# First three attention steps placed among the last value products, modulation terms spread, and separate places for stacked q and k

## The chip, the core and the metric

The kernel runs on one core of a Trainium2 chip. A core has TensorE (PE; its weight loads are listed as PEld), VectorE (DVE), ScalarE (ACT), GpSimd (POOL) and SyncE (SP), which here issues all DMAs. The metric is device time in microseconds (us) of one execution, as a median of several; less is better.

## What is computed

One layer of a backbone block over 512 latent tokens and 256 context tokens, width 1024, all in fp32:

```
sh1, sc1, g1, sh2, sc2, g2 = split(silu(c) @ w_mod + b_mod, 6)
h, hc = modulate(rms_norm(x), sh1, sc1), modulate(rms_norm(ctx), csh1, csc1)
qa, ka, va, hy, qd, kd, vd = split(h @ w_in)          # context rows: k and v only
yd = (softmax(q1 k1) - lam * softmax(q2 k2)) vd       # 4 heads, two components of 64
ya = softmax(qa ka) va                                # 4 query heads on 2 key heads
yh = x2 * conv(h2, x1 * conv(h1, v))                  # long convolutions of 256 channels
x = x + g1 * (concat(rms_norm each of ya, yh, yd) @ w_out)
x = x + g2 * ((gelu(dwconv3(a)) * v) @ w_down)        # a, v = split(modulate(rms_norm(x), sh2, sc2) @ w_up)
```

Queries are 512 rows, keys 768 (256 of the context, 512 latent). The last four parts of the modulation vector (g1, sh2, sc2, g2) are needed only behind the attention.

## The kernel before

**Numbers.** Nearly every product is three matmuls (lines 80 to 83): an operand is split into a high part (ScalarE cast, line 70) and a low remainder (line 78), and hi*hi, hi*lo and lo*hi are summed in PSUM. Scores do it in two matmuls: q and k are transposed to one row per channel, and their high and low halves are stacked along the 128 partitions, so that `ks` (high k twice) and `kz` (low k beside zeros) each need one pass.

**Stages.** Modulation and filters; Hyena projection and convolutions; the q, k and v projections, eight chunks of 256 columns (line 722, `corder`), chunks 6 and 7 the values of the differential heads; attention; output projection; feed-forward. A chunk has two halves of the contraction (`u`), and in each half a block of 12 matmuls for every 128 rows (`b`, `j`): chunk 7 has twelve such blocks.

**Orders.** Outside the blocks marked `manual_schedule` a planner orders each engine's instructions by its own model of time, so an engine's order need not be that of the program. Inside such a block the named engines keep the order of the program. The attention is such a block for TensorE, VectorE and ScalarE (line 1067); the projections are not. Every engine works its list strictly in order, SP's DMA issues included.

**Modulation terms.** Each of the four later parts is a group of eight terms: `mod2_step` (line 694) loads 512 KB of `w_mod` and adds them to `macc` (VectorE, lines 706 and 708; two load buffers, one accumulator). The call after a group's eighth term does the column sums (`due`, 16 small matmuls, line 713, into `mc`) and goes on with the next group. Three groups run beside the projections, two calls ahead of each half chunk from the fourth on (line 730), and the fourth beside the feed-forward stage.

**Preparation of a head.** `prepare` (line 662) transposes q and k, splits them, and stacks them by DMA on SP: four transfers of 128 KB for q (lines 614 to 617) and four of 192 KB for k (line 654). Head 0 is prepared ahead of chunk 6, into the tiles that later hold the attention's outputs (`y`); the others during the attention. There the unstacked q and the unstacked k of a head share one buffer (tag `qk`, lines 608 and 630).

**Attention steps.** A step is 128 queries of one head; the differential heads have four steps each and two score tiles per step. Step n does its scores (`front`: lines 831 and 832, then maximum on VectorE, line 837, and exponential on ScalarE, line 839), mixes the two components of step n - 1 (`combine`, POOL lines 976 and 977), transposes the probabilities of step n - 3 and multiplies those of step n - 5 by the values. Head i + 1 is prepared from the steps in `PREP_AT`; the two Hyena outputs (`y_out`) are transposed at `HY_AT`. The output weights (`wo_unit`, line 1032) go through three raw tiles, tag `wr`, which the projections used before.

In PSUM (8 banks) the projections have three banks of tag `a`, three of `t`, and two of `p`, used by the early modulation and filters and then by the convolution (lines 112 and 516).

## Time and profile before

| | us |
|---|---|
| median of 3 runs | 823.11 (821.0 to 825.92) |
| the profiled execution | 824.9 |
| its span, first to last instruction | 823.1 |
| mean granted TensorE clock | 0.987 of full speed |

The span is what the engines' rows cover; 1.8 us of the execution lie around it. In a timeline row stand start, duration, engine, line of the kernel, operation, output and inputs, shape, and in brackets how long the engine was idle ahead of it and what ended that. Tile names carry their use: `q7L`, `q7C` are the sums of chunk 7 (latent and context rows), `sd02` the scores of head 0, query block 2, `mxd..` their maxima, `pd..` the exponentials, `Td..` the transposes, `yd` the products with the values; `qTd`, `kT0d` the transposes of q and k, `qhld`, `khd` their unstacked halves, `qsd`, `ksd` the stacked ones; `mraw` is a modulation load. Names leave buffer numbers out, and a matmul's row lasts longer than the distance to the next, since matmuls overlap.

### The profile page before, as it was taken

To read this page: it belongs to the slowest core of one execution; us is meant where nothing else is said; L and a number is where in the kernel's file an instruction comes from. 1 tells how busy PE (TensorE), PEld (TensorE's weight loads), DVE (VectorE), ACT (ScalarE), POOL (GpSimd) and SP (SyncE) were. 2 spreads that over 40 slices of the span, in tenths; PEclk is the share of its full clock that TensorE was granted. 3 is DMA by queue.
4 is the path that set the end of the run, shared out by engine and by line. 5 is a ranking of instruction groups with operands and counts; after the bars stand their busy time and mean duration, and the time that the engine had idled before them with its cause. 6 is when DMAs were issued, how large, how long until landed. Compare 5 with 4: busy or idle time off the path is not lost.

```text
span 823.1 us, 11104 instructions
## 1 busy us (share of the span) xinstructions
PE 780.4 (95%) x4334; PEld 657.2 (80%) x4334; DVE 479.3 (58%) x679; ACT 318.6 (39%) x546; POOL 204.0 (25%) x190
## 2 busy tenths in 40 slices
PE   5878999999999788899999999999999999999997
PEld 1247899999999677699888988888888888888886
DVE  4855578886766677678477595344443334333325
ACT  1554424323221477678444263323332233322320
POOL 0652406848841267613043000000000000000000
PEclk9998999999999899999999999999999999999999
DMA  8902232124668232212073173332223233232202
GB/s 326 382 1 88 67 127 78 52 78 137 217 232 247 57 81 57 64 26 78 27 256 105 46 260 106 102 103 85 95 102 103 77 102 102 79 103 90 89 26 102
DMA packets 30701, 93.68 MB, mean 114 GB/s; under 512 B 5639, under 2 KB 8022, under 8 KB 29625
## 3 DMA queue, kind: packets, MB, share of 16 engines
q1 hardware_dynamic: 30649, 92.98, 34.0%
q8 instruction: 34, 0.56, 0.3%
q14 instruction: 18, 0.15, 0.1%
HBM read 83.79 MB, written 2.10 MB: 104 GB/s over the span
## 4 chain that ended last, share of the span: by engine, by line
PE 75%; DVE 6%; DMA 5%; ACT 3%; POOL 2%; issue 2%; SPq 0%; ACTq 0%; DVEq 0%; POOLq 0%
PE u L82 5%; PE u L81 5%; PE u L83 5%; PE dn L82 5%; PE dn L83 5%; PE dn L81 5%; DMA mraw<-in_dram 4%; PE uv L81 2%; PE uv L82 2%; PE ua L83 2%; PE uv L83 2%; PE ua L81 2%; PE ua L82 2%; PE o L82 2%; PE o L81 2%; PE o L83 2%
## 5 line engine op out<-in xcount | busy, mean ns | idle before, releaser
L78 DVE TENSOR_TENSOR ul<-ur,uh 128x1024 fp32r<-128x1024 f32 x62 | 75.9, 1224 | 101.9 <-ACT uh L70 101.1
L70 ACT CAST uh<-ur 128x1024 fp32r<-128x1024 f32 x66 | 69.2, 1051 | 115.7 <-PE u L82 91.0
L81 PE MATMUL u<-h2h,uh 128*128 128x512 f32 (+1 forms) x224 | 81.1, 362 | 0.0
L83 PE MATMUL u<-h2h,ul 128*128 128x512 f32 (+1 forms) x224 | 80.3, 359 | 0.0
L82 PE MATMUL u<-h2l,uh 128*128 128x512 f32 (+1 forms) x224 | 80.3, 359 | 0.0
L82 PE MATMUL dn<-ul,gh 128*128 128x512 f32 x176 | 69.6, 396 | 0.0
L83 PE MATMUL dn<-uh,gl 128*128 128x512 f32 x176 | 69.6, 396 | 0.0
L81 PE MATMUL dn<-uh,gh 128*128 128x512 f32 x176 | 69.3, 396 | 0.0
L78 DVE TENSOR_TENSOR gl<-gT,gh 128x512 fp32r<-128x512 f32 x22 | 15.2, 690 | 60.1 <-ACT gh L70 60.1
L81 PEld LDWEIGHTS u<-h2h,uh 128*128 128x128 f32 x224 | 42.2, 189 | 6.3
L82 PEld LDWEIGHTS u<-h2l,uh 128*128 128x128 f32 x224 | 42.3, 189 | 6.2
L83 PEld LDWEIGHTS u<-h2h,ul 128*128 128x128 f32 x224 | 42.2, 189 | 6.2
L708 DVE SCALAR_TENSOR_TENSOR macc<-mraw,sv,macc 128x1024 f32<-128x1024 f32 x28 | 36.9, 1318 | 14.4 <-DMA mraw<-in_dram 14.2
L78 DVE TENSOR_TENSOR wl<-wr,wh 128x1024 fp32r<-128x1024 f32 x22 | 31.1, 1415 | 21.6 <-ACT wh L70 21.5
L70 ACT CAST gh<-gT 128x512 fp32r<-128x512 f32 x22 | 13.5, 620 | 70.1 <-PE dn L82 70.1
L83 PEld LDWEIGHTS dn<-uh,gl 128*128 128x128 f32 x176 | 33.1, 188 | 8.1
L81 PEld LDWEIGHTS dn<-uh,gh 128*128 128x128 f32 x176 | 33.1, 188 | 8.1
L82 PEld LDWEIGHTS dn<-ul,gh 128*128 128x128 f32 x176 | 33.1, 188 | 8.1
L70 ACT CAST wh<-wr 128x1024 fp32r<-128x1024 f32 x22 | 22.9, 1046 | 40.2 <-issue 11.0
L81 PE MATMUL uv<-h2h,uh 128*128 128x512 f32 x80 | 31.3, 391 | 0.2 <-ACT uh L70 0.2
L81 PE MATMUL ua<-h2h,uh 128*128 128x512 f32 x80 | 31.4, 393 | 0.0
L83 PE MATMUL ua<-h2h,ul 128*128 128x512 f32 x80 | 31.2, 390 | 0.0
(756 smaller groups left out, 2190.6 us busy)
## 6 DMA issues: line engine op xcount, KB each, us to landing
ur<-in_dram SPq DMA_DIRECT2D x66, 512.0 KB, 3.2
mraw<-in_dram SPq DMA_DIRECT2D x32, 512.0 KB, 4.4
wr<-in_dram SPq DMA_DIRECT2D x22, 512.0 KB, 3.3
mraw<-in_dram SPq DMA_DIRECT2D x8, 1024.0 KB, 7.8
or<-in_dram SPq DMA_DIRECT2D x8, 512.0 KB, 3.7
xo<-in_dram SPq DMA_DIRECT2D x6, 512.0 KB, 8.9
ksd<-khd SPq DMA_DIRECT2D x12, 192.0 KB, 3.2
qsd<-qhld SPq DMA_DIRECT2D x16, 128.0 KB, 2.3
```

What stands on the lines that cost most here:

```text
L70: return S.copy(dst, src)
L78: return e.tensor_tensor(dst, src, f(hi), ALU.subtract)
L81: i0 = T_.matmul(o, ah, bh, start=start, stop=False)
L82: T_.matmul(o, ah, bl, start=False, stop=False)
L83: return i0, T_.matmul(o, al, bh, start=False, stop=stop)
L708: V.scalar_tensor_tensor(m2s["a"], r, sv[:, k:k + 1], m2s["a"], ALU.mult, ALU.add)
```

## The change

- Scores and exponentials of steps 0 to 2 (`EARLY`), six score tiles, are issued among the twelve blocks of chunk 7, one after every second block, together with head 1's preparation, the three mixes and the last four modulation terms; for that chunk TensorE and VectorE now follow the order of the program. The attention loop starts at step 3.
- The six tiles use tag `p`, which becomes one place of two banks; the two early users of it, and P and M of each convolution, become halves of one tile.
- Modulation: no calls ahead of the halves of chunk 7; the call after a group's last term does nothing (`pause`), the next does the column sums. In the feed-forward stage the last call moves from block 18 to 20.
- Stacked q and k: one set in the raw weight tiles and the `x` tile (heads 1 and 3), one in its own place (head 2 and the first attention pair), a place for the second pair's q; the unstacked halves have two buffers.
- The Hyena outputs are started at steps 5 and 6 in place of 2 and 3. Two weight tiles become halves of one.

```diff
+EARLY = 3
+MOD_AT = (0, 0, 0, 2, 2, 2, 2, 2, 2, 2, 2, 2, 2, 2, 0, 0)
-PREP_AT = (0, 4, 7, 12, 17)
+PREP_AT = (4, 7, 12, 17)
-HY_AT = (2, 3)
+HY_AT = (5, 6)
...
     def pp(name):
-        return psB.tile([P, 512], F32, tag="p", bufs=2, name=name)
+        return psB.tile([P, 1024], F32, tag="p", bufs=1, name=name)
...
-    mps = pp("modc")
+    modl = pp("modl")
+    mps, l1 = modl[:, :512], modl[:, 512:]
...
-        PM = {"P": Bank(pp(f"P{order}")), "M": Bank(pp(f"M{order}"))}
+        pm = pp(f"PM{order}")
+        PM = {"P": Bank(pm[:, :512]), "M": Bank(pm[:, 512:])}
...
+    def set_of(i):
+        w = i % 2
+        if w not in sets:
+            if w:
+                q, *z = [wp.tile([P, 1024], F32R, tag="wr", bufs=3, name=f"X{j}") for j in range(3)]
+                k = wx.tile([P, 2, 1024], F32R, tag="x", bufs=1, name="ksX")
+                q, k = q.rearrange("p (a c) -> p a c", a=2), [k[:, j, :768] for j in range(2)]
+                z = [t[:, :768] for t in z]
+            else:
+                q = att.tile([P, 2, T], F32R, name="qsY")
+                k = att.tile([P, 2, 768], F32R, name="ksY")
+                z = att.tile([P, 2, 768], F32R, name="kzY")
+                k, z = [k[:, j] for j in range(2)], [z[:, j] for j in range(2)]
+            for j in range(2):
+                G.memset(f(z[j][64 - 64 * j:128 - 64 * j]), 0.0)
+            sets[w] = q, k, z
+        return sets[w]
+
+    def unstacked(i, name):
+        if i == 1:
+            return tmp.tile([P, 1024], F32R, tag="b", bufs=4, name=name)
+        return att.tile([P, 1024], F32R, tag="qk", bufs=2, name=name)
...
-            qhl = att.tile([P, 2, T], F32R, tag="qk", bufs=1, name="qhl" + name)
-            qs = att.tile([P, 2, T], F32R, tag="qs", bufs=2, name="qs" + name)
+            qhl = unstacked(i, "qhl" + name).rearrange("p (a c) -> p a c", a=2)
+            qs = set_of(i)[0] if i < 5 else att.tile([P, 2, T], F32R, name="qsZ")
...
+            kh = unstacked(i, "kh" + name)[:, :768]
+            _, ks, kz = set_of(i)
...
     def mod2_step():
+        if m2s.pop("pause", False):
+            return
...
-            m2s["due"] = due
+            m2s["due"], m2s["pause"] = due, True
...
+    def early_step(e):
+        n, jj = divmod(e, 2)
+        if n >= EARLY:
+            return
+        qs, (ks, kz) = prepared[0]["q"], prepared[0]["k"]
+        s = pp(f"se{n}{jj}")
+        scores(s, qs, ks, kz, jj, n)
...
+        exp_of(p_, mx, s, state["st0"][:, n, jj:jj + 1])
+        held[n].append(p_)
...
-            for _ in range(2 if 2 * ci + u > 2 else 0):
+            for _ in range(MOD_AT[2 * ci + u]):
                 mod2_step()
+            if ci == 7 and u == 0:
+                order = tc.manual_schedule(engines={mybir.EngineType.PE, mybir.EngineType.DVE})
+                order.__enter__()
+                nextp = prepare(1, pt)
...
+                    if ci == 7:
+                        e = 6 * u + 2 * b + j
+                        if e % 2 == 0:
+                            early_step(e // 2)
+                        if e in (4, 8):
+                            early_mix(e // 4 - 1)
+                        if e % 3 == 0:
+                            mod2_step()
+                        if e > 3:
+                            next(nextp, None)
+            if ci == 7 and u == 1:
+                for _ in nextp:
+                    pass
+                early_mix(EARLY - 1)
+                while m2s["n"] < m2s["end"] or "due" in m2s:
+                    mod2_step()
+                order.__exit__(None, None, None)
...
-    n = 0
+    n = EARLY
...
-            start(prepare(PREP_AT.index(n) + 1, ps_t))
+            start(prepare(PREP_AT.index(n) + 2, ps_t))
...
-        if 2 <= i < 20 and i % 2 == 0:
+        if 2 <= i <= 20 and i % 2 == 0:
             mod2_step()
```

`early_mix(n)` does for step n what `combine` does in the loop; of the early probabilities the first component goes to a tile of tag `y`, the second to one of tag `b`.

More of the change, by code (lines that the diff above doesn't have):

```diff
@@ L599, in rows_of, with stack_q @@
         return t.rearrange("p a c -> p (a c)")[:, :n]
-    def stack_q(name, tiles, ps, early, res):
+    jobs = [("d", h) for h in range(4)] + [("a", b) for b in range(2)]
+    prepared = [{} for _ in jobs]
+    sets = {}
+    def set_of(i):
[19 more added lines that the diff above has]
+        return att.tile([P, 1024], F32R, tag="qk", bufs=2, name=name)
+    def stack_q(i, name, tiles, ps):
+        res = prepared[i]
         t0 = ps("qT" + name)
@@ L619, in stack_q, with stack_k @@
         yield
-    kzs = []
-    def stack_k(name, tiles, ps, early, res):
-        if early:
-            kh, *ks, kz0, kz1 = (rows_of(y_tile(f"{n}{name}"), 768) for n in ("kh", "ks0", "ks1", "kz0", "kz1"))
+    def stack_k(i, name, tiles, ps):
+        res = prepared[i]
+        if i == 0:
+            kh = rows_of(res.pop("kh"), 768)
+            *ks, kz0, kz1 = (rows_of(y_tile(f"{n}{name}"), 768) for n in ("ks0", "ks1", "kz0", "kz1"))
             kz = [kz0, kz1]
@@ L629, in stack_k @@
         else:
[L630 to L640 removed]
+            kh = unstacked(i, "kh" + name)[:, :768]
+            _, ks, kz = set_of(i)
         for half in range(2):
             t0 = ps(f"kT{half}" + name)
[L643 to L644 removed]
+            for n in range(3):
+                T_.transpose(t0[:, n * P:(n + 1) * P], tiles(3 * half + n), ident)
             sl = slice(half * 384, half * 384 + 384)
@@ L804, in block_kernel @@
                     hi_of(t[:, kt0:kt0 + 2, :], b2[:, :, cs], "v" if i else "a")
-    while m2s["n"] < m2s["end"] or "due" in m2s:
-        mod2_step()
     close(m2)
@@ L1010, in values @@
         if tt % 2 and hf_ == 1 and j != 0:
-            start(finish_d(h, yps, state["rr", i]) if kind == "d" else finish_a(h, yps))
+            start(finish_d(h, yps, state[f"rr{i}"]) if kind == "d" else finish_a(h, yps))
     running = []
```

119 lines of the change are left out of this document (56 added, 63 removed).

## The prediction

> **What bounds the kernel now.** I first read the head of the page, then the stretches around the change, then the engines' timelines, and last the waits. The page:
>
> ```profile
> span 823.1 us, 11104 instructions
> PE 780.4 (95%) x4334; PEld 657.2 (80%) x4334; DVE 479.3 (58%) x679; ACT 318.6 (39%) x546; POOL 204.0 (25%) x190
> ```
>
> The stretches (length, busy time of PE, PEld, DVE, ACT and POOL, granted TensorE clock, DMA share, GB/s):
>
> ```profile
> 248.80:266.10 17.30, 17.22 (x146) 17.01 (x144) 10.94 (x14) 2.11 (x5) 1.49 (x3) 1.00 0.86 251
> 266.10:271.70 5.60, 3.24 (x16) 3.25 (x17) 1.95 (x3) 1.61 (x2) 1.44 (x2) 0.73 0.06 23
> 271.70:283.90 12.20, 8.73 (x39) 6.81 (x40) 8.04 (x15) 5.87 (x13) 3.19 (x3) 0.84 0.19 43
> ```
>
> TensorE is the bound over the whole span (95%), so a change pays where TensorE stands or crawls. The last value products (248.8 to 266.1) fill it and leave ScalarE idle for 15 of 17 us. Then come 5.6 us with only 16 matmuls and 12.2 us with 39, at a reduced clock. The timeline shows why:
>
> ```profile
> 248.77 0.28 PE L81 MATMUL q7L<-wh,hTh 128*128 128x256 f32 x1
> ...
> 265.74 0.28 PE L83 MATMUL q7C<-wh,cTl 128*128 128x256 f32 x1
> 268.46 3.40 PE L713 MATMUL mc<-ones,macc 128*128 128x2 f32 x16 [2.44 <-DVE macc L708]
> 271.72 0.77 PE L831 MATMUL sd00None<-ks0d,qsd 128*128 128x512 f32 x1
> ...
> 275.49 0.50 PE L831 MATMUL sd01None<-ks0d,qsd 128*128 128x512 f32 x1
> ...
> 276.28 0.49 PE L644 MATMUL kT0d<-ident,kd 128*128 128x128 f32 x3
> ...
> 283.90 0.50 PE L831 MATMUL sd03None<-ks0d,qsd 128*128 128x512 f32 x1 [1.32 <-ACT pd02None L839]
> ```
>
> The products end at 266.02. TensorE waits 2.44 us for the last modulation term, does its column sums, and starts step 0 of the attention (sd00) at 271.72; step 3 (sd03) starts at 283.90. Steps 0 to 2 have only scores and exponentials, no transposes of probabilities and no values, so nothing fills TensorE while the maximum and the exponential run. From the end of the products to step 3 pass 283.90 - 266.02 = 17.9 us.
>
> **The change part by part, first the moved steps.** What goes into the value products, with its prices at full clock:
>
> ```profile
> 220.88 1.84 PE L713 MATMUL mc<-ones,macc 128*128 128x2 f32 x16
> 222.58 0.37 PE L82 MATMUL q5L<-wl,hTh 128*128 128x256 f32 x1
> ...
> 243.97 0.63 PE L604 MATMUL qTd<-ident,qd 128*128 128x128 f32 x4
> 244.44 0.49 PE L644 MATMUL kT0d<-ident,kd 128*128 128x128 f32 x3
> ```
>
> and on VectorE and ScalarE:
>
> ```profile
> 273.45 0.96 DVE L837 TENSOR_REDUCE mxd00None<-sd00None 128x1 f32<-128x768 f32 x1 [1.19 <-PE sd00None L832]
> ```
>
> ```profile
> 274.45 0.90 ACT L839 ACTIVATE pd00None<-sd00None,mxd00None 128x768 f32<-128x768 f32 x1 [6.72 <-DVE mxd00None L837]
> ```
>
> - The products keep 266.02 - 248.77 = 17.25 us.
> - Six score tiles of four matmuls each: one takes 276.28 - 275.49 = 0.79 us from its start to the next instruction, so 4.7 us.
> - The ten transposes of head 1: 0.47 us for the four of q (243.97 to 244.44), and by that rate 0.35 us for each three of k, so 1.2 us.
> - The column sums of the third group: 222.58 - 220.88 = 1.7 us, where they now take 3.26 us at the reduced clock.
>
> Sum 24.85 us: without any wait, step 3 would start at 248.77 + 24.85 = 273.6, which is 10.3 us earlier than 283.90.
>
> **What of it can wait.** All six early tiles share one PSUM place (two banks, tag p), so each one waits until the exponential of the tile before has read it. That loop is 0.79 us of scores, about 0.1, 0.96 of maximum, 0.1, 0.90 of exponential, about 0.1: 3.0 us. Between two early tiles lie two blocks of twelve products, 17.25 / 12 x 2 = 2.9 us, and the next scores fall due 0.8 us after the scores before plus these 2.9. So the loop fits with 0.7 us to spare if VectorE and ScalarE answer at once. ScalarE will. VectorE is now in an order written out by hand, and the early maxima stand behind the modulation terms, which wait for their loads:
>
> ```profile
> 254.81 1.28 DVE L708 SCALAR_TENSOR_TENSOR macc<-mraw,sv,macc 128x1024 f32<-128x1024 f32 x1 [0.39 <-DMA mraw<-in_dram]
> 259.87 1.28 DVE L708 SCALAR_TENSOR_TENSOR macc<-mraw,sv,macc 128x1024 f32<-128x1024 f32 x1 [3.77 <-DMA mraw<-in_dram]
> ```
>
> These are terms 19 and 20 of 24 (counted from 0); the change puts term 19 ahead of the block and 20 behind the first maximum, near 252 us. If their loads land as now, the first maxima wait, the second score tile comes 4 to 6 us late, and TensorE stands that long. Against that: in the stretch from 248.8 DMA moves 251 GB/s, because the stacking of head 0, an early load of output weights and the modulation loads run together. After the change the three tiles of raw weights hold head 1's stacks, so the output weights cannot be loaded there, and head 0's stacking comes out of the way of the terms' column sums in program order, so it can run earlier. In the block are then four loads of 512 KB and head 1's eight stacking transfers (4 x 128 and 4 x 192 KB), 3.3 MB in 25 us or 130 GB/s. SP issues a stack in 0.6 to 0.9 us (rows at rival 1), and a load queued behind a stack that waits for VectorE waits with it; that is inside the bound. Bounds: 0 if the loads keep up, 6 us if they land as now; I take 2.5, nearer to 0 since the traffic halves. Step 3 at 276.1, gain 7.8 us.
>
> VectorE's other work in the block (a weight split, head 1's splits, three mixes) and POOL's (two memsets, three mixes) runs on engines with 6 and 16 us free in that stretch; I cost it at nothing, and if the cover fails it is part of these 6 us.
>
> **A place each for stacked q and k.** Before, the unstacked q and k of a head share one buffer, so ScalarE, in its fixed order, stands before a cast until the stacking transfer has read the buffer. Its waits, in us, times and longest:
>
> ```profile
> ACT khd L70 <- DMA qsd<-qhld: 3.1, 2, 1.6
> ACT qhld L70 <- DMA ksd<-khd: 2.1, 1, 2.1
> ```
>
> and TensorE in the same stretch (290 to 315 us):
>
> ```profile
> PE kT0d L644 <- ACT atd10None L70: 1.4, 1, 1.4
> PE ynd L862 <- DVE mxd21None L837: 1.2, 1, 1.2
> PE kT1d L644 <- ACT atd02None L70: 0.5, 1, 0.5
> PE kT1d L644 <- ACT atd10None L70: 0.5, 1, 0.5
> ```
>
> With two buffers these three ScalarE waits, 5.2 us, go. What TensorE loses behind them is 1.4 + 1.2 + 0.5 + 0.5 = 3.6 us. What is late next is VectorE, or head 2's own stacks, which step 8 reads hardly a step and a half after they are issued. Bounds 0 and 5.2; I take 3.5, by the TensorE rows.
>
> **Moves at no net cost.** First the ScalarE half of one Hyena output, then the last read of head 3's stacks and the first use of the output weights:
>
> ```profile
> 284.11 0.85 ACT L880 ACTIVATE Y<-yTh,cols 128x256 fp32r<-128x256 f32 x2
> ```
>
> ```profile
> 341.86 0.28 PE L832 MATMUL sd33None<-kzd,qsd 128*128 128x256 f32 x1
> ```
>
> ```profile
> 371.44 1.04 ACT L70 CAST oh<-or 128x1024 fp32r<-128x1024 f32 x1
> ```
>
> The Hyena outputs move from steps 2 and 3 to steps 5 and 6; of the two, the one at step 3 leaves the part that I count, and both enter it later, beside head 2's preparation. So 0 if they fit beside other work, +1.7 us (2 x 0.85) at worst, and -0.85 at best; I take 0. The merged PSUM places of the convolution and of the first products: each half had a reader ahead of it already; 0. The raw output weights can now be loaded only after 341.86, when head 3 frees the shared tiles; 29 us lie from there to their first use at 371.44, both move together, and a load of 512 KB takes the 3.7 us of this row of the DMA issues:
>
> ```profile
> or<-in_dram SPq DMA_DIRECT2D x8, 512.0 KB, 3.7
> ```
>
> So it is hidden. If SP's queue held it past that use, behind head 5's stacking, ScalarE would stand in its fixed order for the rest. The fourth group's column sums move two blocks of up-products later in the feed-forward stage, well ahead of their use at the end; 0.
>
> **Sum.** 7.8 + 3.5 = 11.3 us. The profiled execution took 824.9 us with a span of 823.1; the three runs have a median of 823.11, within 0.3% of it, so I set the difference against that: 811.8, say 812.
>
> **The rivals.**
> 1. Head 0's stacks come as late as now, so the first early scores wait. These rows have the k stacks issued from 250.05 and 251.34, and a landing after 6.3 us:
>
> ```profile
> 250.05 1.24 SPq L654 DMA_DIRECT2D ks0d<-khd  x2
> 251.34 1.72 SPq L654 DMA_DIRECT2D ks1d<-khd  x2
> ```
>
> ```profile
> ks0d<-khd SPq DMA_DIRECT2D x2, 192.0 KB, 6.3
> ```
>
> The first tile needs ks0, so it can start near 256.5, where it falls due at 250.2: 6.3 us in place of the 2.5. For it: nothing but program order moves them. Against: head 0's inputs are long ready. Time: 823.1 - 4.0 - 3.5 = 815.6.
> 2. The attention gives nothing: the three ScalarE waits turn into waits for VectorE, and the Hyena outputs land in the fullest steps (+1.7). For it: the 1.2 us at ynd name VectorE. Against: the other three gaps name ScalarE. Time: 823.1 - 7.8 + 1.7 = 817.0.
> 3. Slower: the waits at the one score place put TensorE on half clock in the value products. The trace has this: after a gap of 2.44 us, the 16 column sums took 3.40 us where they took 1.84, and the clock was 0.73 and 0.84 in the two stretches. If each turn of the loop had a gap like that, everything in the block would run at half clock: 248.8 + 2 x 24.85 = 298.5 in place of 283.9, and 298.5 - 283.9 - 3.5 = 11.1 us slower, 834. It decides from a loop of 3.8 + 2.4 = 6.2 us on, twice the 3.0 worked out; all four terms in the block would have to come late.
> 4. It does not do what it says: the planner, which orders what is not ordered by hand, takes the 11.3 us back ahead of the block or behind it: 823.1. For it: orders of VectorE, POOL and SP outside the block shift with every edit. Against: the stages behind are held by TensorE, which has nothing new to wait for.
>
> [...]
>
> **How the numbers follow.** Forecast 812 with a chance of 0.56; rival 1 (815.6) 0.14; rival 2 (817) 0.11; rival 4 (823) 0.11; rival 3 (834) 0.08. Lowest: no wait in the block, all 5.2 us and 0.85 more: 823.1 - 10.3 - 5.2 - 0.85 = 806.8. The range 806 to 820 holds the forecast and rivals 1 and 2, about 0.81. A difference of 0.5% (4 us) is about what a measurement of this kernel can tell from none. Faster by over that, below 819: 0.80; within it 0.12; slower 0.08.
>
> **What would show it.** Right: score tiles between the products of q7, no idle stretch before the column sums, the clock at 1.00 there, step 3 starting near 276, and no ScalarE wait for qsd or ksd behind it. Wrong: a first early score waiting for ks0d (rival 1); maxima waiting for macc and TensorE for the exponentials, with the clock under 1 in the products (rival 3); the same pace of the steps behind step 3 (rival 2).

## The result, and the profile after

| | before | after |
|---|---|---|
| median of 7 runs each, us | 824.29 (821.0 to 825.92) | 818.09 (817.47 to 821.48) |
| ratio of the runs | | 0.9931, 95% interval 0.9909 to 0.9953 |
| the profiled execution, span | 824.9, 823.1 | 818.88, 817.1 |

The change makes the kernel 0.7% faster: 6.2 us by the medians and 6.0 by the spans, where 11.3 were forecast. The time lies inside the range, the sign is right, the gain is about half of the forecast's. First the head of the page after:

```profile
span 817.1 us, 11113 instructions
...
PE 776.7 (95%) x4334; PEld 655.9 (80%) x4334; DVE 476.5 (58%) x679; ACT 318.5 (39%) x546; POOL 201.7 (25%) x190
```

TensorE is busy as large a share of the span as before. The same stretches after the change (length, then busy time of PE, PEld, DVE, ACT and POOL, clock, DMA share, GB/s), and TensorE's rows there:

```profile
248.80:253.50 4.70, 4.70 (x28) 4.70 (x28) 2.12 (x3) 0.00 (x0) 0.00 (x0) 0.64 0.66 212
253.50:277.90 24.40, 22.81 (x180) 21.89 (x179) 18.58 (x25) 9.52 (x18) 6.08 (x4) 1.00 0.53 162
277.90:279.70 1.80, 1.80 (x19) 1.80 (x18) 0.61 (x3) 1.25 (x3) 0.38 (x2) 1.00 0.16 43
```

```profile
247.97 2.18 PE L737 MATMUL mc<-ones,macc 128*128 128x2 f32 x16 [1.87 <-DVE macc L732]
...
253.51 0.28 PE L83 MATMUL q7L<-wh,hTh 128*128 128x256 f32 x1
...
259.43 0.50 PE L745 MATMUL se<-ks1d,qsd 128*128 128x512 f32 x1 [0.79 <-ACT pe L750]
...
264.04 0.50 PE L745 MATMUL se<-ks0d,qsd 128*128 128x512 f32 x1 [0.81 <-ACT pe L750]
...
278.00 1.85 PE L737 MATMUL mc<-ones,macc 128*128 128x2 f32 x16
279.71 0.48 PE L745 MATMUL sd03None<-ks0d,qsd 128*128 128x512 f32 x1
```

The reader is to see three things. The block itself does what it should: from chunk 7's first product (253.51) to step 3 (279.71) it takes 26.2 us at full clock, with two waits of 0.8 us; before, the same span took 283.90 - 248.77 = 35.1 us. But it begins 4.7 us later than before, and not at 248.77 as the forecast had it: 1.3 us of this are there already at chunk 3's first product (192.42 against 191.11), and in chunk 6 the second group's column sums now wait 1.87 us, and behind these the clock is 0.64. So step 3 gains 283.90 - 279.71 = 4.2 us and not 7.8.

The two waits of 0.8 us in the block come from VectorE, where the maxima (`mxe`) stand behind terms; term 20 waits for its load:

```profile
256.21 1.28 DVE L732 SCALAR_TENSOR_TENSOR macc<-mraw,sv,macc 128x1024 f32<-128x1024 f32 x1
257.40 0.95 DVE L749 TENSOR_REDUCE mxe<-se 128x1 f32<-128x768 f32 x1
...
260.75 1.28 DVE L732 SCALAR_TENSOR_TENSOR macc<-mraw,sv,macc 128x1024 f32<-128x1024 f32 x1 [1.21 <-DMA mraw<-in_dram]
261.95 0.95 DVE L749 TENSOR_REDUCE mxe<-se 128x1 f32<-128x768 f32 x1
```

Behind step 3 (starts of first instructions; "last sums" are the last value products of the attention, `ya`, "last output" the last transpose `yTa`):

| stretch, us | before | after | gain | forecast |
|---|---|---|---|---|
| start to step 3 | 283.90 | 279.71 | 4.2 | 7.8 |
| step 3 to the last attention's first scores | 64.95 | 62.30 | 2.65 | 3.5 |
| from there to the last sums | 50.25 | 49.45 | 0.8 | 0 |
| last sums to last output | 9.68 | 11.34 | -1.7 | 0 |
| last output to the end | 414.3 | 414.3 | 0 | 0 |

In the second stretch the Hyena outputs now stand at steps 5 and 6:

```profile
285.88 0.51 PE L745 MATMUL sd11None<-ksX,X 128*128 128x512 f32 x1 [0.35 <-ACT pd10None L750]
...
287.12 0.62 PE L940 MATMUL yTh<-ident,yhn 128*128 128x128 f32 x4
...
290.44 0.55 PE L1055 MATMUL Td02None<-ident,pe 128*128 128x128 f32 x3 [1.14 <-ACT atd02None L72]
...
293.16 0.60 PE L940 MATMUL yTh<-ident,yhn 128*128 128x128 f32 x4
...
296.55 0.55 PE L1055 MATMUL Td03None<-ident,pd03None 128*128 128x128 f32 x3 [1.75 <-ACT atd02None L72]
...
298.04 0.58 PE L745 MATMUL sd13None<-ksX,X 128*128 128x512 f32 x1
```

Step 5 to step 7 (sd11 to sd13) takes 12.2 us, where it took 300.75 - 291.82 = 8.9; TensorE waits 1.14 and 1.75 us for the casts `atd`, which ScalarE does behind the outputs. In the last but one stretch VectorE has a new instruction in its way:

```profile
394.29 2.58 DVE L80 TENSOR_TENSOR ol<-or,oh 128x1024 fp32r<-128x1024 f32 x1
396.80 0.67 DVE L997 TENSOR_REDUCE sa<-ysqa 128x4 f32<-128x512 f32 x1
...
399.07 0.69 DVE L1006 TENSOR_TENSOR yna<-yna,sa 128x512 f32<-128x512 f32 x1 [1.40 <-POOL sa L196]
```

```profile
399.91 0.63 PE L940 MATMUL yTa<-ident,yna 128*128 128x128 f32 x4 [1.44 <-DVE yna L1006]
```

The split of an output weight (2.58 us, beside GpSimd's own) stands ahead of the sum of squares, and TensorE waits 1.44 us for what follows from that.

### The profile page after: what moved, and what is told of

Read it like the earlier page. It is cut to its first block, busy times and chain, and to the rows that moved or that the text cites. A ratio compares the mean times of both kernels' runs of the same rounds, so it can differ in the third digit from the quotient of the medians.

```text
span 817.1 us, 11113 instructions
## 1 busy us (share of the span) xinstructions
PE 776.7 (95%) x4334; PEld 655.9 (80%) x4334; DVE 476.5 (58%) x679; ACT 318.5 (39%) x546; POOL 201.7 (25%) x190
## 4 chain that ended last, share of the span: by engine, by line
PE 81%; DVE 8%; ACT 4%; POOL 2%; DMA 2%; issue 2%; SPq 0%; ACTq 0%; DVEq 0%; POOLq 0%
PE u L84 5%; PE u L83 5%; PE u L85 5%; PE dn L85 5%; PE dn L84 5%; PE dn L83 5%; PE uv L83 2%; PE ua L85 2%; PE uv L84 2%; PE uv L85 2%; PE ua L83 2%; PE ua L84 2%; PE yd L1072 2%; DMA mraw<-in_dram 2%; PE f L384 2%
## 5 line engine op out<-in xcount | busy, mean ns | idle before, releaser
L83 PEld LDWEIGHTS dn<-uh,gh 128*128 128x128 f32 x176 | 33.1, 188 | 8.1
L84 PEld LDWEIGHTS dn<-ul,gh 128*128 128x128 f32 x176 | 33.1, 188 | 8.1
L84 PE MATMUL uv<-h2l,uh 128*128 128x512 f32 x80 | 31.2, 390 | 0.0
```

Of the source, the lines that this page charges most:

```text
L83: i0 = T_.matmul(o, ah, bh, start=start, stop=False)
L84: T_.matmul(o, ah, bl, start=False, stop=False)
```

## The experiments

Every changed kernel below was timed (4 to 12 runs each) beside the kernel before on the same chip; ratios are to that. Of the kernel before there are two further profiles. The table has each profile's stretches in us: chunk 3's first product (`q3`) to chunk 7's first (`q7`), the block from there to step 3, then the stretches of the table above, and what TensorE lost to a clock under 1.00 between 190 and 440 us (summed over stretches of 2 us: length times one minus clock). The single edits (e1 to e7, e11) are made in the changed kernel; e9, e10 and e13 are made in e6, e12 in e8, e14 in e13 and e15 in e14.

```
run                     ratio (95%)              q3-q7  block  step3-sa  sa-sums  sums-out  clock lost
before                  1                        57.7   35.1   65.0      50.3     9.7       5.1
before, second profile                           57.4   33.1   64.1      49.4     9.7       5.1
before, third profile                            59.4   31.9   64.1      49.5     9.7       5.1
after                   0.9931 (0.9909-0.9953)   61.1   26.2   62.3      49.5     11.3      1.7
e1_sums_block           0.9952 (0.9937-0.9968)   55.7   30.0   63.7      49.4     11.4      3.4
e2_prep_after           0.9976 (0.9963-0.9989)   57.4   32.8   62.3      49.5     11.3      3.4
e3_hyena_late           0.9926 (0.9910-0.9943)   59.3   26.3   59.1      52.3     11.3      3.4
e4_split_after          0.9915 (0.9901-0.9930)   59.7   26.2   62.3      49.4     9.7       1.7
e5_own_place            0.9926 (0.9910-0.9942)   60.1   26.7   63.8      50.2     11.3      5.1
e6_stacks_after         0.9921 (0.9903-0.9939)   57.5   29.5   62.7      49.4     11.4      1.7
e7_hyena_2527           0.9895 (0.9879-0.9911)   61.9   26.3   58.1      51.4     11.4      3.4
e8_all_four             0.9877 (0.9861-0.9894)   57.4   30.9   58.7      51.4     9.7       5.1
e9_no_third             0.9868 (0.9830-0.9906)   57.5   22.3   62.9      49.4     11.3      0.0
e10_maxima_first        0.9964 (0.9940-0.9988)   57.5   26.4   65.3      50.1     11.3      3.4
e11_one_qk              1.0006 (0.9982-1.0030)   60.9   26.2   68.2      49.4     11.3      5.1
e12_five                0.9914 (0.9885-0.9943)   57.6   28.8   59.3      51.4     9.7       3.4
e13_third_late          0.9983 (0.9964-1.0003)   57.4   22.3   62.9      52.4     9.7       3.4
e14_third_late_all      0.9931 (0.9908-0.9953)   57.4   22.3   58.7      54.5     9.7       3.4
e15_sums_36             0.9907 (0.9875-0.9939)   57.9   22.4   58.7      57.0     9.7       0.0
```

Read down a column: a stretch that an edit doesn't touch repeats to 0.1 us in most rows (49.4, 11.3, 22.3), so a larger difference in it is mostly the edit or a spell of slow clock. The first column is the exception: six rows that have the change's own chunks 3 to 6 differ from 59.3 to 61.9, with waits of 0.8 to 2.0 us at the column sums in chunk 6. So a single profile tells the lateness of chunk 7 to 2 us at best; the rows of changed kernels without such a wait lie at 57.4 to 57.9 (55.7 where the sums moved out of chunk 6).

**Why chunk 7 begins late.** Two ways to take the wait out of chunk 6. The first moves the second group's column sums into the block:

```diff
-            m2s["due"], m2s["pause"] = due, True
+            m2s["due"], m2s["pause"] = due, (1, 5, 0, 0)[g]
...
-                        if e % 3 == 0:
+                        if e % 3 != 2:
                             mod2_step()
```

> The second group's column sums move from chunk 6 into the block (five paused calls in place of one after that group), and the eight terms of the third group are called in the block, eight of its twelve steps, so that no term of that group runs in chunk 6. Theory: the 1.87 us that TensorE waits in chunk 6 at the column sums (247.97 us) and the half-rate products behind it (250 to 252.7 us, 0.21 us a product in place of 0.12) both come from this one wait, and together cost 3.2 to 3.6 us. Then the first product of chunk 7 starts 5.0 us earlier than 253.5 (these 3.3 and the 1.7 us of the sums, which now lie in the block), near 248.5 to 249.0, the granted clock from 245 to 255 is 1.00, and step 3 of the attention starts 3 us earlier, near 276.5, if the block's maxima don't wait for more loads than now (1.6 us of waits). Rival: the products of chunk 6 are late for another reason (the first 60 us, or the ten transposes of head 0 that now stand early); then chunk 7 starts only 1.7 us earlier, near 251.8, and step 3 is where it was, 279.7. Second rival: eight loads in the block make the maxima wait as the prediction's bound said (4 to 6 us); then step 3 comes at 279 to 282 though chunk 7 starts early.

`pause` now counts the calls that do nothing. Chunk 7 begins at 248.88 (the starts given in this part are those of the first instruction on TensorE's timeline of the run) and the clock is 1.00 up to 276 us: besides the 1.8 us of the sums, which only moved, the lateness in chunk 6 was the wait and what followed from it. But step 3 comes at 278.91, and the time is no better than the change's: the block takes 30.0 us, with the sums that moved into it, and its own column sums wait for the eight terms that now all lie in it:

```profile
276.54 2.51 PE L738 MATMUL mc<-ones,macc 128*128 128x2 f32 x16 [2.15 <-DVE macc L733]
```

The second moves head 0's preparation behind the calls of chunk 6:

```diff
-        if ci == 6:
-            for _ in prepare(0, pt):
-                pass
         for u in range(2):
             for _ in range(MOD_AT[2 * ci + u]):
                 mod2_step()
+            if ci == 6 and u == 0:
+                for _ in prepare(0, pt):
+                    pass
```

> Head 0's transposes, casts and stacking are moved behind the calls of the terms of chunk 6, as they stood before the change, and nothing else is changed. Theory: the stacks of head 0 ahead of the loads of terms 14 and 15 on the DMA queue make these terms late (243.5 and 246.5 in place of 239.5 us); without them ahead, the last term of the second group comes near 241 us, its column sums don't wait, the clock stays 1.00, and chunk 7 starts near 250.1 (248.77 of before plus the 1.3 us by which the first 190 us are late). What it costs: the first score tile waits for the stacks of k, which now stand behind two more loads: step 3 may gain less than 3.3 us, or lose up to 5. Rival: the terms are late because the pause and the new spread put them later, and not because of the stacks; then the column sums still wait over 1 us, and chunk 7 starts after 252.

VectorE's last two terms of that group, first after the change, then in this run:

```profile
243.53 1.29 DVE L732 SCALAR_TENSOR_TENSOR macc<-mraw,sv,macc 128x1024 f32<-128x1024 f32 x1 [3.48 <-DMA mraw<-in_dram]
...
246.54 1.28 DVE L732 SCALAR_TENSOR_TENSOR macc<-mraw,sv,macc 128x1024 f32<-128x1024 f32 x1 [0.59 <-DMA mraw<-in_dram]
```

```profile
239.01 1.28 DVE L732 SCALAR_TENSOR_TENSOR macc<-mraw,sv,macc 128x1024 f32<-128x1024 f32 x1 [1.78 <-DMA mraw<-in_dram]
241.22 1.28 DVE L732 SCALAR_TENSOR_TENSOR macc<-mraw,sv,macc 128x1024 f32<-128x1024 f32 x1 [0.93 <-DMA mraw<-in_dram]
```

Term 15 is done 5.3 us earlier, the sums don't wait, and chunk 7 begins at 249.63. So head 0's early preparation, which the change allows, made them late, in two ways. After the change the load of term 14 is issued at 236.73, among the eight stacking transfers (233.41 to 239.38), and takes 6.4 us to land, where those of the run with the preparation moved take 3.2. And VectorE does head 0's splits ahead of term 13, so the buffer that term 15 needs comes free, and its load is issued, at 240.07 in place of 237.26. The price of moving the preparation is rival 1 of the prediction, seen here pure:

```profile
257.38 0.77 PE L745 MATMUL se<-ks0d,qsd 128*128 128x512 f32 x1 [6.16 <-DMA ks1d<-khd]
```

This row of TensorE's timeline in the same run shows 6.16 us of waiting for the stacks of k, where rival 1 had 6.3; the block takes 32.8 us.

Between the two: only the eight transfers are moved, behind the load of term 15. (The planner then also put the splits of head 0's k on VectorE behind term 13, so this run does not tell the transfers and the splits apart.)

```diff
+        m2s["load"] = dma(r, wmod2[g, k])
...
+            ready = m2s["load"].ins
...
+        with tc.issue_after(ready) if i == 0 else nullcontext():
+            dma(f(qs[0:64, 0]), f(qh[0:64]))
...
```

> The eight stacking transfers of head 0 are issued behind the load of the last term of the second group (term 15), and nothing else is asked for. Theory: on the DMA queue the stacks delay these loads; behind them, term 15 is done near 241.5 us, the column sums in chunk 6 don't wait (0.8 to 1.9 us now), the clock stays 1.00, and the time from chunk 3's first product to chunk 7's first falls from 59.3 to 61.1 us to 57.4; and since the stacks are still issued by 243 us, the block stays as it is, 26.2 us from chunk 7's first product to step 3. Time: 2 us less than the changed kernel, near 816. Rival: stacks behind the terms land after chunk 7 has begun, and the first score tile waits (as it did with all of head 0's preparation moved, where the block took 32.8 us); then the block takes 28 us or more and the time is 818 or over.

The theory is right up to chunk 7, which begins at 249.99 with the sums done by 247.2 and no wait. And it gains nothing: step 3 comes at 279.46. TensorE now waits in the block, for the stacks no longer, but for an exponential whose maximum stands behind terms that wait for their loads, and behind a weight split (VectorE's timeline, then TensorE's):

```profile
250.33 0.76 DVE L733 TENSOR_SCALAR macc<-mraw,sv 128x1024 f32<-128x1024 f32 x1 [2.93 <-DMA mraw<-in_dram]
...
254.38 1.29 DVE L735 SCALAR_TENSOR_TENSOR macc<-mraw,sv,macc 128x1024 f32<-128x1024 f32 x1 [1.21 <-DMA mraw<-in_dram]
255.58 1.22 DVE L81 TENSOR_TENSOR wl<-wr,wh 128x1024 fp32r<-128x1024 f32 x1
256.72 0.95 DVE L752 TENSOR_REDUCE mxe<-se 128x1 f32<-128x768 f32 x1
```

```profile
258.75 0.50 PE L748 MATMUL se<-ks1d,qsd 128*128 128x512 f32 x1 [3.64 <-ACT pe L753]
```

The block takes 3.3 us more than after the change: 2.0 us are waiting (3.64 against 0.79 + 0.81) and 1.2 us more busy time of TensorE, with a spell of slow clock at 260 us (0.50 from 260 to 262). Chunk 7 began 3.5 us earlier, but term 18 is added only 1.8 us earlier (254.38, after the change 256.21), term 20 only 0.7 us (260.04 against 260.75). That made a new theory: the loads pace the block.

**What paces the block.** The same without the third group (its terms and sums are left out):

```diff
-    m2s = {"n": 0, "pl": m2, "end": 3 * NK}
+    m2s = {"n": 0, "pl": m2, "end": 2 * NK}
...
```

> As the run with head 0's stacks behind the load of term 15, and without the third group of the modulation: its eight terms and its column sums are left out (its column is zero, so the output differs). Theory: with the stacks moved, chunk 7 began 3.5 us earlier and its end stayed where it was, because the maxima stand behind modulation terms whose loads come every 2.5 to 3 us; the loads pace the block, not TensorE. Without terms the block takes what the prediction added up without waits, less the column sums: 24.85 - 1.7 = 23.2 us from chunk 7's first product to step 3, against 29.5 us with them, and the time is 6.3 us less than 819.0, near 812.5. Rival: the loop of scores, maximum and exponential through the one score place (3.0 us for one tile against 2.9 us of products) or the stacks of head 0 hold the block; then it still takes 26 us or more, and the time is 815 or over.

The stretch from chunk 7's first product to step 3 in this run (columns as above):

```profile
252.06:274.40 22.34, 22.34 (x181) 21.84 (x180) 11.47 (x19) 9.70 (x19) 5.53 (x4) 1.00 0.24 57
```

TensorE is busy for all of the 22.34 us, at full clock, though the loop through one score place is there as before and the DMA share is 0.24. The time falls by 0.5% more than with the stacks alone. So the one score place was no bound, and the third group was. In the twelve profiles of changed kernels that have its terms in or ahead of the block, chunk 7 begins anywhere from 248.9 to 254.1, and step 3 comes from 277.0 to 282.5 without following that start; in the four without them, chunk 7 begins from 249.5 to 252.1, and step 3 comes from 271.8 to 274.4.

What this leaves open is which part of a term counts: its load, its 1.28 us on VectorE, or the two load buffers. SP's own waits at the loads (after the change, 249 to 265 us; us, times, longest) name mostly the term that frees a buffer:

```profile
SPq L727 <- DVE macc L732: 8.8, 5, 3.1
...
SPq L727 <- DMA mraw<-in_dram: 2.4, 4, 0.8
```

So load and term wait for each other in turn. A third load buffer, which would tell, was not tried.

Then the terms put otherwise, the first two maxima ahead of them:

```diff
-MOD_AT = (0, 0, 0, 2, 2, 2, 2, 2, 2, 2, 2, 2, 2, 2, 0, 0)
+MOD_AT = (0, 0, 0, 2, 2, 2, 2, 2, 2, 2, 2, 2, 2, 0, 0, 0)
-                        if e % 3 == 0:
+                        if e in (3, 4, 6, 7, 8, 9):
                             mod2_step()
```

> As the run with head 0's stacks behind the load of term 15, with the terms of the block set otherwise among the maxima: two terms fewer before the block, and in the block six calls after the second maximum in place of four from the first on, so that the first two maxima stand ahead of the terms that wait for loads. All work is done. Theory: the block's wait was that of the first maxima for loads; the block then takes 24.85 us and 0.5 to 2 us of waits (29.5 in the run before), chunk 7 still begins near 250, step 3 comes near 276.5 and the time is 3 us less than 819.0, near 816. Rival: the loads pace all terms, and what the first maxima no longer wait the last column sums do; then TensorE waits 2 us or more at these, and step 3 stays at 279.

The block falls to 26.4 us, as the theory has it, and step 3 comes at 277.01. But the time rises (0.9964 against 0.9921): of this profile's gain of 3 us 2.7 are lost again between step 3 and the last attention, a stretch with two spells of slow clock (278 to 283 us, 0.50 in the middle, and 340 to 343 us, down to 0.56). What sets these off is not shown. A miss.

And the whole third group in the late attention, where few transfers run (after the change a DMA share of 0.16 from 342.0 to 391.5 us, 0.51 in the block; one call at each of eight steps, the sums behind the out-projection's first products; the room is taken from tag `y3`, two buffers in place of three):

```diff
+            if n in (17, 19, 21, 23, 29, 31, 33, 35):
+                mod2_step()
...
+    m2s.pop("pause")
+    m2s.pop("due")()
```

> As the run with head 0's stacks behind the load of term 15, with the third group's eight terms and its column sums moved out of the block: the terms go one each to steps 17, 19, 21, 23, 29, 31, 33 and 35 of the attention, behind the splits of the step, the column sums behind the out-projection's first products; the place for the finished heads has two buffers in place of three to make room. All work is done. Theory: the block then takes 22.3 us as without the terms (29.5 with them in it), TensorE's clock doesn't fall in it, and the terms cost little where VectorE waits for TensorE anyway and few transfers run: 0 to 3 us. Time: 3 to 6 us less than 819.0 (0.992 of before), so 0.984 to 0.988. Rival: VectorE is 75 to 85% busy in those steps and stands on the chain of each; every term then costs TensorE up to 1.28 us, and the 10 us of terms give back 6 us or more: 0.991 or over.

The block takes 22.3 us and nothing is left out, 7 us less than with the terms in it, and the time is no better than before the whole change. The profile says where the gain goes: 3.0 us at the terms (49.4 to 52.4; the smaller room is in this too), 1.8 at the sums, and behind these, on TensorE's timeline:

```profile
407.72 1.84 PE L740 MATMUL mc<-ones,macc 128*128 128x2 f32 x16
...
413.13 0.80 PE L85 MATMUL o<-ol,Y 128*128 128x512 f32 x1 [1.94 <-POOL ol L81]
...
417.57 0.63 PE L86 MATMUL o<-oh,Y 128*128 128x512 f32 x1
```

1.94 us for an output weight's split and then half rate (0.43 us from product to product, 0.23 before). The weight's tile lies where the modulation's tiles lay and comes free with the sums. With the sums at step 36, in a kernel that also has the other edits shown below (own place, outputs later, split behind the last output):

```diff
+            if n == 36:
+                m2s.pop("pause")
+                m2s.pop("due")()
```

> The run with the third group in the late attention and the other edits, with the third group's column sums at step 36, among the last value products, in place of behind the out-projection's first products. Theory: the weights 3 and 4 of the out-projection lie where the modulation's tiles lay, so they come free with the sums 20 us earlier; TensorE doesn't wait for the split of weight 3 (1.94 us), the clock doesn't fall at 410 us, and the time is 4 to 5 us less: 0.9931 becomes 0.987 to 0.9885, as good as the combined run without this edit (0.988). Rival: the weights come late because of their loads behind those of the terms on the DMA queue; then TensorE still waits over 1 us near 410 and the time stays at 0.991 or over.

The wait and the half rate at 410 are gone (0.23 us from product to product from 408 us on; the stretch from the last output to the end is 414.3 us again, after 421.8 in the run below), and the profiled span is 811.6 us, the shortest of all. But its six runs spread from 812.6 to 821.1, and the interval (0.9875 to 0.9939) reaches from the best to no better than the change; its worth stays open. The run that it was made from, with the sums behind the out-projection's first products as in the diff before:

> The same with own place for l1, the Hyena outputs at steps 25 and 27 and the split of weight 4 behind the last output (the combined run without the third group in the block). If the costs are apart from each other: the combined run's 0.988 less 0.004 to 0.007, so 0.981 to 0.984, near 810. Rival: Hyena outputs and terms meet in the same steps and the time is no better than the combined run's, 0.987 or over.

0.9931, no better than the change: the rival's time, but not its reason. The outputs and the terms don't disturb each other (54.5 us in this stretch is 49.4 and the 2.0 and 3.0 us of each alone); what takes the gain is the stretch behind the last output, 421.8 us in place of 414.3, and the run with the sums at step 36 shows that their place does it.

**The Hyena outputs.**

```diff
-HY_AT = (5, 6)
+HY_AT = (18, 20)          # e3; e7: (25, 27)
```

> The two Hyena outputs move from steps 5 and 6 to steps 18 and 20, where one score tile a step and the split values fill TensorE. Theory: at steps 5 and 6 they delay ScalarE and VectorE ahead of the casts of the transposed probabilities (TensorE idle 1.14 and 1.75 us), and the stretch from step 5 to step 7 (sd11 to sd13) took 12.2 us against 8.9 before; without them it takes 9 to 9.8 us, and the two outputs cost 1 us of TensorE time where they now stand. Time: 2 us less than the changed kernel, near 816. Rival: the stretch is long because of the new places of stacked q and k or of head 2's preparation at the same steps; then it stays over 11.5 us and the time rises by the 1 us that the outputs cost, near 819.

> The two Hyena outputs at steps 25 and 27, in the quiet end of the attention, where TensorE is full and no head is being finished or prepared. Theory: an output costs 2.2 us at step 5 or 6, where it stands in the loop of transposes, casts, maximum and exponential, and only its 0.47 us of TensorE time where TensorE is full. Then step 5 to step 7 takes 7.7 us as with steps 18 and 20, the stretch from the first score tile of the last attention (sa) to its last values takes 49.5 + 1.0 = 50.5 us (52.3 with steps 18 and 20), and the time is 3.5 us less than the changed kernel, near 814.5. Rival: each output costs 1 us or more wherever it stands, since a later engine has to wait for it; then that stretch takes over 51.5 us and the time is 816.5 or more.

In the second of the two, steps 5 to 7 and then the two outputs on TensorE's timeline:

```profile
286.08 0.51 PE L745 MATMUL sd11None<-ksX,X 128*128 128x512 f32 x1 [0.35 <-ACT pd10None L750]
...
293.76 0.58 PE L745 MATMUL sd13None<-ksX,X 128*128 128x512 f32 x1
```

```profile
363.96 0.66 PE L940 MATMUL yTh<-ident,yhn 128*128 128x128 f32 x4 [0.97 <-DVE Y L950]
...
369.30 0.64 PE L940 MATMUL yTh<-ident,yhn 128*128 128x128 f32 x4
```

Step 5 to step 7 takes 7.7 us in both runs, 4.5 less than after the change: an output costs 2.2 us at those steps. Where TensorE is full (busy for 49.1 of the 49.5 us after the change) it costs 1 us (51.4 against 49.4 for two), which is more than its 0.5 us of transposes; here the rival was nearer. At steps 18 and 20 the same stretch is 2.9 us longer, but a spell of slow clock from 334 to 338 us (0.56 and 0.58), ahead of the outputs (342 and 350 us), lies across its start and takes 0.7 us of this; that leaves 1.1 us an output, about as at steps 25 and 27. Steps 25 and 27 make the kernel 0.4% faster than the change as it was.

**The second unstacked buffer.**

```diff
-        return att.tile([P, 1024], F32R, tag="qk", bufs=2, name=name)
+        return att.tile([P, 1024], F32R, tag="qk", bufs=1, name=name)
```

> The changed kernel with one buffer in place of two for the unstacked q and k of a head. Theory (the prediction's term): ScalarE again stands before a cast until the stacking transfer has read the buffer, and the second buffer is worth 3.5 us: the time is 821.5, and from step 7 to step 10 (sd13 to sd22) it takes 16 us where it now takes 13.0 (16.2 before). Rival: these waits lie beside others (the loop of the step, VectorE), and the second buffer is worth under 1.5 us; then the stretch takes under 14.5 us and the time is under 819.5.

The view of the waits names ScalarE's `khd`, which waits once, 2.3 us, for the transfer that reads the buffer; then TensorE's timeline, and 8 us of it by the windows (columns as above):

```profile
ACT khd L72 <- DMA qsY<-qhld: 2.3, 1, 2.3
```

```profile
292.63 0.90 PE L1055 MATMUL Td02None<-ident,pe 128*128 128x128 f32 x3 [3.58 <-ACT atd02None L72]
...
295.53 0.99 PE L745 MATMUL sd12None<-ksX,X 128*128 128x512 f32 x1
```

```profile
290.00:298.00 8.00, 5.37 (x20) 4.64 (x21) 2.62 (x6) 2.96 (x7) 0.92 (x1) 0.57 0.00 1
```

The time is that of the kernel before: without this buffer the whole change is worth nothing. The cost isn't mainly where either theory put it (step 7 to step 10 takes 14.1 us against 13.0) but at step 5, where the wait of 2.3 us for head 2's stack of q stands ahead of the Hyena output and the cast `atd`, TensorE stands for 3.58 us (1.14 after the change), and the clock is 0.57 over the next 8 us. It is 5.9 us in all, while the clock loses 3.4 us more than after the change; how much of the 5.9 is the clock's is not separated.

**The split of an output weight.**

```diff
+            state["fin"] = V.scalar_tensor_tensor(l, t0[:, sl], gc, f(h), ALU.mult, ALU.subtract)
...
+        if n_ == 4:
+            with tc.issue_after(state["fin"].ins):
+                lo_of(l, r, h, WO_LO[n_])
...
```

> VectorE's split of output weight 4 is made to follow the last output of the attention; nothing else is changed. Theory: this split (2.58 us on VectorE at 394.3 us, beside GpSimd's split of weight 3 at 393.4 us) stands ahead of the sum of squares of the last normalisation and makes TensorE idle 1.44 us at 399.9 us; behind it, that idle time falls to 0.1 us or less, and the time is 1.4 us less than the changed kernel, near 816.7. Rival: the normalisation waits for GpSimd (the power behind its own split, which ends at 395.8 us) or for ScalarE; then the idle time stays over 1 us and the time is the same, 818.

The first output transpose on TensorE's timeline of this run:

```profile
398.38 0.60 PE L940 MATMUL yTa<-ident,yna 128*128 128x128 f32 x4
```

The wait of 1.44 us is gone, and the stretch is 9.7 us again, as before the change. 1.6 us in the profile; the ratio (0.9915) differs by less than the intervals.

**The first stage.** All profiles of the change begin chunk 3 later than the first profile of the kernel before did (191.5 to 194.6 against 191.1).

```diff
-    mps, l1 = modl[:, :512], modl[:, 512:]
+    mps, l1 = modl[:, :512], pt("l1")
```

> The column of absolute sums (l1) gets a PSUM place of its own (tag t) again instead of the second half of the tile that holds the first modulation's products; the order of every engine stays as in the changed kernel. Theory: in the changed kernel VectorE's read of l1 (hbias) waits for the modulation products that write the other half of the same tile (0.4 to 2.0 us in four profiles of it; it began at once before), and everything behind it in the first stage is late by 0.4 to 1.3 us. With an own place hbias begins within 0.1 us of the end of the splits ahead of it, the transposes of the modulation (modT) come at 53.5 to 54.3 us, where they came at 53.7 to 56.2 in five executions of the first stage of the changed kernel and at 54.0 before, and the time is 1 us less, near 817. Rival: the first stage differs by chance from one execution to the next (its transfers and its clock); then hbias starts at once but modT still lies anywhere from 53.7 to 56.2, and the time is 818.

> The kernel before, profiled once more. Theory of chance: the end of the first stage (the transposes of the modulation, modT) lies anywhere from 53.7 to 57.1 us as in the changed kernel's executions, and the first product of chunk 3 follows it by 137.1 us (137.2 to 138 in the changed kernel). Theory of the change: it lies at 54.0 again, within 0.3 us.

> As the run before it: by chance the modulation's transposes come anywhere from 53.7 to 57.1 us; by the change they come at 54.0 again, within 0.3 us. [...]

With a shared tile VectorE's read of l1 does wait for the modulation's products (0.4 to 2.1 us); with its own place it doesn't. But modT came at 56.8 us, later than without it, and at 53.8 to 55.2 in the later runs that have this edit too. The two new profiles of the kernel before have 54.06 and 54.73. So the first stage differs by up to 3.4 us between kernels whose first stage is written alike (53.7 to 57.1), the wait is hidden in that, and whether the change makes the stage later by the 0.85 us between the means (54.28 of three, 55.13 of eleven) stays open. The three profiles of the kernel before also have blocks of 35.1, 33.1 and 31.9 us, since the last column sums waited 2.44 us in the first and 1.43 and 1.32 in the others: the forecast was made against the slowest of the three.

**Together.** Own place, stacks behind the load, outputs at steps 25 and 27 and the split behind the last output:

> All four edits together: own place for l1, stacks behind the load of term 15, Hyena outputs at steps 25 and 27, split of weight 4 behind the last output. If the four costs are apart from each other, their sum holds: 1 + 2 + 3.5 + 1.4 = 7.9 us less than the changed kernel, near 810. Rival: a part is given back where the next wait stands (the block's maxima behind their loads, the tail of the attention); then the time is 812 to 814.

> The four edits of the combined run (own place for l1, stacks behind the load of term 15, Hyena outputs at steps 25 and 27, split of weight 4 behind the last output) and the maxima ahead of the terms. If the block's wait is what the combined run still lost, its 815.7 falls by 3 us to near 812.7, that is 1.5% under the kernel before. Rival: it is given back at the last column sums or in the attention, and the time stays over 814.5.

The four make 0.9877: 1.2% faster than the kernel before, and the interval lies wholly under that of the change; of the kernels that do all the work it is the fastest with a narrow interval. By the sum of the four costs, 7.9 us, it should have been 0.9835, another 3.5 us lower: the stacks' part is given back in the block (30.9 us against 26.2). The maxima ahead of the terms don't help here either.

## Where the prediction held and where it failed

- **The block's own size held.** 24.85 us without waits were worked out, 23.15 without the column sums; without the third group it took 22.34. That it fits through one score place held: without the terms TensorE didn't wait once there.
- **The step that failed: "What of it can wait", and the start under it.** The sum was 248.77 + 24.85 + 2.5 = 276.1 for step 3; it came at 253.51 + 26.2 = 279.71. The waits in the block were even less than the 2.5 us taken (1.6). What failed is the start, taken over from the kernel before as if nothing ahead of it moved. The text counted head 0's early stacking as a help alone ("so it can run earlier"); the runs show that this early preparation made terms 14 and 15 late, and that the column sums in chunk 6 waited for them, with a spell of slow clock behind (0.64). 3.4 of the 4.7 us lie there; the other 1.3 are there before chunk 3, and their cause stays open.
- **Nor was the wait a size of its own.** Where the start was mended, the block took longer (29.5 us with the transfers behind the load, 32.8 with the whole preparation moved), since the terms and the stacks did not come earlier by as much. A wait added to a moving start was the wrong sum; the times at which the terms come give the end. The text had the mechanism (maxima behind terms, bounds 0 and 6) and put term 20 near 252, where it came at 260.75.
- **"Moves at no net cost" was wrong twice.** The Hyena outputs cost 4.5 us at steps 5 and 6 (0 taken, 1.7 the upper bound, from ScalarE's time alone; the chain through TensorE, ScalarE and VectorE counts). The output weights cost 1.6 us, not by their loads, which were weighed, but by a split that the planner set into VectorE's list.
- **The second buffer was worth more than 3.5,** 5.9 us in the changed kernel, over the bound of 5.2, in a profile that also lost more to the clock (5.1 us against 1.7). With the outputs' 4.5 us against it, step 3 to the last attention came out at 2.65 us; against the two further profiles of the kernel before it is 1.8.
- **Rivals.** 1 (stacks late) did not happen, and the run with the preparation moved shows what it would have cost. 2 was right about the fullest steps and wrong about the buffer. 3 named slow clock behind thin stretches; in the changed kernel it came in chunk 6 (0.64) and not in the block (1.00), and in the block only in some of the experiments (0.50 at 260 us with the transfers behind the load). 4 happened in part: the split of weight 4 is a place that the planner chose.
- **The baseline.** The forecast was made against a profile with a spell of slow clock at 346 us (0.50 from 348 to 350) that the two others don't have (1.00 from 340 to 354). It accounts for the 0.8 us gained behind the first scores of the last attention, which are no gain of the change, and for about as much ahead of them.

## What to carry to other kernels

When work is moved into a stretch, ask which engine's list it joins and what paces that list; a wait counted from a start that the change can move is no term of a sum, but the time at which the late thing comes is. Take the paced work out for one run: that shows in a single number whether the stretch is bound by it. A move "at no cost" is to be read at its new place through the whole loop of engines, and a planner's list is to be compared behind the change and not only at it.

## What was not expected of the hardware

**The clock was lost in fixed portions.** In 19 profiles TensorE's loss between 190 and 440 us is 0, 1.7, 3.4 or 5.1 us and nothing between. The kernel with the Hyena outputs at steps 18 and 20 has such a portion behind a wait of only 0.79 us with sixteen column sums (TensorE's timeline, then the windows):

```profile
245.98 1.92 PE L737 MATMUL mc<-ones,macc 128*128 128x2 f32 x16 [0.79 <-DVE macc L732]
```

```profile
248.00:250.00 2.00, 2.00 (x15) 2.00 (x15) 0.77 (x2) 0.00 (x0) 0.00 (x0) 0.73 0.32 94
250.00:252.00 2.00, 2.00 (x11) 2.00 (x11) 1.71 (x2) 0.96 (x2) 0.00 (x0) 0.50 0.65 246
252.00:254.00 2.00, 2.00 (x16) 1.92 (x15) 1.61 (x2) 1.64 (x2) 0.00 (x0) 0.92 0.72 260
```

(0.27 + 0.50 + 0.08) x 2 = 1.7 us, as much as 3.4 us at the 0.50 of the middle row lose. The same sums without a wait (1.84 us, chunk 5) took none in any profile. The third profile of the kernel before has such a portion (244 to 250 us) behind a wait of only 0.15 us:

```profile
243.22 1.95 PE L713 MATMUL mc<-ones,macc 128*128 128x2 f32 x16 [0.15 <-DVE macc L708]
```

But the run with the sums at step 36 lost none behind the same sums with waits of 0.22 and 0.54 us, so such a wait can have a portion behind it and need not. Nor does the same code lose it each time (346 us in the kernel before: 1.7 us in the first profile, none in the two others). What sets the size of a portion, and when one comes, is not shown. For the price of a wait it means that 0.79 us had 1.7 us of lost clock behind it, 3.64 us (transfers behind the load) 1.7, and 3.58 us (one buffer) 3.4.

The price is not always paid. Step 3 to step 4 of the kernel before, in its second profile and in its first, takes the same time at 0.60 and at full clock; at full clock TensorE is idle for 1.25 us of it, at 0.60 for none:

```profile
281.63:285.95 4.32, 4.32 (x18) 3.79 (x18) 3.65 (x9) 2.98 (x8) 2.88 (x3) 0.60 0.65 156
```

```profile
283.90:288.23 4.33, 3.08 (x19) 2.35 (x19) 4.14 (x9) 2.99 (x8) 2.88 (x3) 1.00 0.65 156
```

So the last column of the table of runs is a loss of clock and not always one of time.

**Two splits at once.** The same split of 128x1024 on VectorE took 2.58 us beside GpSimd's (393.4 to 395.8 us), and the two others 1.23 alone; moved behind the last output, the first took 1.22 us too, at 403.29 (shortest, median, longest of three in nanoseconds, after):

```profile
L80 DVE TENSOR_TENSOR ol<-or,oh x3: 1225/1226/2583, 394.3 to 412.3; 128x1024 fp32r<-128x1024 f32 x3
```
